# Applying the norm factor after the expert products instead of before them

## The chip, the cores and the metric

One Trainium2 chip; the kernel runs on one of its cores. The metric is the device time of one execution in microseconds (us). Engines: TensorE (PE, with its weight loads as PEld), VectorE (DVE), ScalarE (ACT), GpSimd (POOL) and SyncE (SP), which here only issues DMA.

## The reference

One encoder layer over 512 tokens of width 1024, float32. The first half is attention in three head groups, an output projection `w_out` and a residual. The second half, which the change is about, in short:

```
x = x + mix @ w_out                     # (512, 1024), called x1 in the kernel
h = x * rsqrt(mean(x*x) + eps) * g_ffn  # RMS norm: one factor r per token, one gain per column
group, two experts of 8 in the group, and two gates per token, from h @ w_r1, h @ w_r2
for each token and each of its two experts e (32 experts):
    a = silu(h @ w1[e]) * (h @ w3[e])   # w1, w3: 1024 x 512
    x += gate * (a @ w2[e])             # w2: 512 x 1024
```

The factor r is one number per token, so (r * x) @ w = r * (x @ w): it may be applied to rows before the products or to their results behind them.

## The kernel before, in words

**Attention and output projection.** The first 355 us compute the three head groups. The product with `w_out` is made in eight pieces (row block `a` of 128 tokens, column half `n`); three are issued before routing, the last five (`LISTED`) inside it.

**Routing** (`route`, lines 1101 to 1277). For each of four row blocks `a`: `add_x` adds the projection to `x1` (DVE); `square` sums squares (ACT); `rows` turns x1 on PE (`turn_x`), copies it (`copy`, ACT), multiplies by the router weights (`logits_x`, PE, line 1132), and computes the factor r with `rstd_ops` into `rst[:, 3, a]`. `full` (line 1149) makes the normed rows `xr = r * x1` on ACT, and `store` writes them to the DRAM tile `xd` from POOL's DMA queue. `xr` lives in the granules `k0` (blocks 0 and 1) and `va` (blocks 2 and 3), which attention has left. `choose` picks group and experts on DVE, ranks tokens within experts on PE, and gives every token-expert pair a slot: expert pair `pr` (experts pr and pr + 16) has 128 slots, 64 for each. `first_gather` multiplies `xr` by the one-hot matrix `G` on PE and so gathers the first 512 columns of pair 0's rows without a DMA. `table` builds on PE the list of tokens and gates by slot. The one-hot comparisons and the small operations ahead of `table` are on POOL for blocks 0 to 2 and on DVE for block 3.

These steps are tasks of a planner (`task`, `run_tasks`): each has an engine, a cost in us and its dependencies; the planner takes next the task that can start soonest and, among equals, the one with the longest way to the end. It fixes the order on each engine only. At run time every engine goes through its list in that order and waits for what each instruction needs.

**Experts** (line 1334 to the end). For each of 16 expert pairs: `up` multiplies the 128 gathered rows by w1 and w3 (PE, line 1406, the two experts of a pair on the two halves of the array), silu on ACT (line 1462), the product with the w3 result on DVE (line 1475), four transposes and the copy `uT` (ACT, line 1482), the product with w2 (line 1494), the gate, and `combine`, which adds the results to x1 through one-hot products (lines 1421 to 1424). `turn_rows` turns the rows of the next pair on PE. These rows come from `xd` by an indirect DMA of POOL (`rows_load`, line 1367), two pairs ahead; `rows_in` has two buffers.

**Weights.** The experts' 192 loads of 1 MB each are issued on SP in a fixed order by `load_w`, into a ring of 21 buffers named in `RING`; load n takes the buffer of load n - 21 and waits until it is free. Nine loads are issued during the output projection, twelve behind `route`, two more before the first pair, then two after every four k steps of products. SP issues in order: a load that waits for its buffer holds those behind it. The first nine are places `w` to the second `g` of the ring. Pair 0's half `up_half(0, 0, 0)` uses loads 1 and 2.

An overflow branch at the end (an expert with more than 64 tokens) reads `xd` too; it isn't entered with this input.

Of the kernel before, what the change touches and what calls it, by code (L numbers as in the profile page):

```python
# [12 lines left out]
F32 = mybir.dt.float32  # L13
# [4 lines left out]
AF = mybir.ActivationFunctionType  # L18
ALU = mybir.AluOpType
# [4 lines left out]
P = 128  # L24
S = 512
D = 1024
KT = D // P
# [5 lines left out]
F = 512  # L33
EPS = 1e-6
NEG = -1e30
RING = "w b q k2 k1 h h g g v f m m h h d e j k k0 va".split()
LN_EXP = [s.name for s in SETS].index("natural_log_exp_and_others")

NA_KEYS = ((64, 248), (0, 248), (0, 248), (0, 192))
# [5 lines left out]
def tile_encoder(ctx: ExitStack, tc, x, mem, g_mix, g_mem, g_ffk, w_in, w_kv, w_out, gains,  # L45
                 na_tab, dil_tab, w_r, b_r, w1, w3, w2, out):
    nc = tc.nc
    V = nc.vector
    cst = ctx.enter_context(tc.tile_pool(name="cst", bufs=1))
    drp = ctx.enter_context(tc.tile_pool(name="drp", bufs=1, space=DR))  # L50
    gov = drp.tile([S, NE], F32, name="gov")
    xd = drp.tile([S, D], F32, name="xd")
    man = ExitStack()
    man.enter_context(tc.manual_schedule())

    def xtile(name, n=D):
# [11 lines left out]
        name=nc.get_next_instruction_name(), engine=mybir.EngineType.Activation, ins=[], outs=[],  # L68
# [5 lines left out]
    ident = cst.tile([P, P], F32, name="ident")  # L74
# [6 lines left out]
    def granule(kind, name, dt=F32):  # L81
        return big.tile([P, 4, 512], dt, name=name, tag=kind, bufs=BUFS[kind])
# [800 lines left out]
    q = pt("warm")  # L883
# [12 lines left out]
    q = rows_turn(0)  # L896
# [117 lines left out]
    x1 = xtile("x1")  # L1014
# [4 lines left out]
    def small(name, shape, dt=F32):  # L1019
        return rk.tile(shape, dt, name=name)  # L1020
# [7 lines left out]
    rst = small("rst", [P, 4, 4])  # L1028
# [20 lines left out]
    def G_tile():  # L1049
        return rk.tile([P, 4, P], F32, name="G", tag="G", padded_shape=[P, 8, P])  # L1050

    xr, xr2, Gs, first_x = [], [], [], []


    class Task:
# [9 lines left out]
    def task(eng, dur, fn, *deps):  # L1065
        tasks.append(Task(eng, dur, fn, deps))
        return tasks[-1]
# [31 lines left out]
    LEAD = 1.0  # L1099

    def route():
        x_done, sq_done, lgt_done, free_lg, tb_done, pt_free, rl_done, mb_done, wop_prev, f_done = {}, {}, {}, {}, {}, [], {}, {}, [], {}

        parts, last_p, x_got = {}, [], {}

# [8 lines left out]
        def rows(a):  # L1114
            st = {}

            def turn_x(n):
                st["q", n] = bank("pt", NPT, "tTp")
                for k in range(4):
                    c = n * 512 + k * P  # L1120
                    nc.tensor.transpose(st["q", n][:, k * P:(k + 1) * P], x1[:, a, c:c + P], ident)

            def copy(n):
                if "tT" not in st:
                    st["tT"] = r3.tile([P, 2, 512], F32, name="tT", tag=("qTm", "kvm")[a % 2])
                nc.scalar.activation(st["tT"][:, n], st["q", n], AF.Copy)

            def logits_x(n):
                if n == 1:
                    st["l"] = bank(f"lg{a % 2}", 1, "rl")  # L1130
                for k in range(4):
                    nc.tensor.matmul(st["l"][:, 0:36], st["tT"][:, n, k * P:(k + 1) * P], wr[:, 4 * n + k, :],
                                     start=(n == 1 and k == 0), stop=(n == 0 and k == 3))
            rl = None
            for n in (1, 0):
                t = task("P", 0.46, lambda n=n: turn_x(n), x_done.get((a, n)), *pt_free[-NPT:][:1] if len(pt_free) >= NPT else ())
                c = task("A", 0.57, lambda n=n: copy(n), t, rl_done.get(a - 2))
                pt_free.append(c)
                rl = task("P", 0.95, lambda n=n: logits_x(n), c, rl, *free_lg.get(a - 2, ()))
            rl_done[a] = rl  # L1140
            s = rst[:, :, a:a + 1]
            r = s[:, 3]
            w = [task("V", 0.07, lambda: V.tensor_add(s[:, 0], sqs[:, a, 0:1], sqs[:, a, 1:2]), sq_done.get((a, 0)), sq_done.get((a, 1)))]
            for eng, dur, f in rstd_ops(s):
                w.append(task(eng, dur, f, w[-1]))
            r_done = w[-1]
            lgt = task("V", 0.17, lambda: V.scalar_tensor_tensor(lg[:, a], st["l"][:, 0:36], r, br, op0=ALU.mult, op1=ALU.add), rl, r_done)

            def full():
                if a % 2 == 0:  # L1150
                    xr2.append(granule(("k0", "va")[a // 2], "xr"))
                xr.append(xr2[a // 2][:, 2 * (a % 2):2 * (a % 2) + 2].rearrange("p a b -> p (a b)"))
                nc.scalar.activation(xr[a], x1[:, a], AF.Copy, scale=r)

            def store():
                nc.gpsimd.dma_start(xd[a * P:(a + 1) * P], xr[a])
            f_done[a] = task("A", 1.1, full, r_done, f_done.get(a - 1))
            task("G", 1.0, store, f_done[a])
            choose(a, lgt)

        def choose(a, lgt):
# [83 lines left out]
            def first_gather():  # L1245
                if a == 0:
                    first_x.append(bank("pj", 2, "xq"))
                for k in range(4):
                    nc.tensor.matmul(first_x[0][:, k * P:(k + 1) * P], xr[a][:, k::KT], Gs[0][:, a],
                                     start=(a == 0 and k == 0), stop=(a == 3), skip_group_check=True)  # L1250
            x_got[a] = task("P", 0.9, first_gather, G_last[-1], f_done[a], x_got.get(a - 1), last_p[0], x_done[LISTED[-2]])

            def table():
                if a == 0:
# [18 lines left out]
        for a in range(4):  # L1273
            block[0] = a
            rows(a)
        task("P", 3.0, lambda: None, x_got[3])
        run_tasks()

# [61 lines left out]
    att_stack.close()  # L1340
    wk_ = moe.enter_context(tc.tile_pool(name="wk", bufs=1, side="right", reuse_waits="tile"))
    rings["v"] = rings["f"] = wk_
    for tag, n, bufs in (("u", 2, 1), ("ringf", 8, 1), ("ringv", 8, 1), ("xT", 2, 4), ("rows", 4, 2), ("uT", 2, 1)):
        for _ in range(bufs):
            wk_.tile([P, n * 256], F32, name="place", tag=tag, bufs=bufs)
    load_w(12)
    ots = rk.tile([P, 2, 4, P], F32R, name="ot", tag="G")

    def scale_x(q, half):
        xT = wk_.tile([P, 4, P], F32, name="xT", tag="xT", bufs=4)  # L1350
        V.tensor_tensor(xT, q, gfk[:, 0, 4 * half:4 * half + 4].unsqueeze(2).to_broadcast([P, 4, P]), op=ALU.mult)
        return xT
# [5 lines left out]
    V.scalar_tensor_tensor(none, tb[0][:, 0:16], -1.0, none, op0=ALU.add, op1=ALU.add)  # L1358
    where_ = small("where", [P, 16], U32)
    V.tensor_copy(where_, none)  # L1360
    rows_in = [wk_.tile([P, D], F32, name="rows", tag="rows", bufs=2) for _ in range(2)][::-1]

    def rows_load(pr):
        if pr < 2:
            nc.gpsimd.memset(rows_in[pr], 0.0)
        if pr < NPAIR:
            nc.gpsimd.indirect_dma_start(out=rows_in[pr % 2], out_offset=None, in_=xd,  # L1367
                                         in_offset=bass.IndirectOffsetOnAxis(ap=where_[:, pr:pr + 1], axis=0),
                                         bounds_check=S - 1, oob_is_err=False)

# [19 lines left out]
    def turn_rows(pr, halves=range(2)):  # L1390
        nxt = []
        for half in halves:
            q = trp("xTp")
            for k in range(4):
                nc.tensor.transpose(q[:, k], rows_in[pr % 2][:, 4 * half + k::KT], ident)  # L1395
            nxt.append(scale_x(q, half))
        rows_load(pr + 2)
        return nxt

# [51 lines left out]
    def gate_half(pr):  # L1451
        if pr:
            p1 = up(pr, 0)
        else:
            p1 = up_tile(0)
            p_first.append(up_tile(1))
            up_half(0, 0, 0, p1)
            up_half(0, 1, 0, p_first[0])
            xT.extend(turn_rows(0, (1,)))
            up_half(0, 0, 1, p1)  # L1460
        u = wk_.tile([P, F], F32, name="u", tag="u", bufs=1)
        nc.scalar.activation(u, p1, AF.Silu)  # L1462
        return u

    def hidden(pr, u):

        nonlocal xT
        while pr == NPAIR - 1 and between:
            between.pop(0)()
        if pr:  # L1470
            p3 = up(pr, 1)
        else:
            p3 = p_first[0]
            up_half(0, 1, 1, p3)
        V.tensor_mul(u, u, p3)  # L1475
        if pr + 1 < NPAIR:
            xT = turn_rows(pr + 1)
        t = trp("uTp")
        for f in range(4):
            nc.tensor.transpose(t[:, f, :], u[:, f::4], ident)  # L1480
        uT = wk_.tile([P, 4, P], F32, name="uT", tag="uT", bufs=1)
        nc.scalar.activation(uT, t, AF.Copy)  # L1482
        while between:
            between.pop(0)()
        return uT
# [83 lines left out]
    with tc.If(flag > 0):  # L1569
        with tc.tile_pool(name="ov", bufs=1) as ov, tc.tile_pool(name="ovps", bufs=1, space=PS) as ovs:  # L1570
            with tc.For_i(0, NE) as e:
# [6 lines left out]
                for a in range(4):  # L1578
                    gv = ov.tile([P, 1], F32, name="gv")
                    nc.sync.dma_start(gv, gov[a * P:(a + 1) * P, bass.ds(e, 1)])  # L1580
                    t = ov.tile([P, D], F32, name="ovt")
                    nc.sync.dma_start(t, xd[a * P:(a + 1) * P])
                    o = ov.tile([P, D], F32, name="ovo")
                    nc.sync.dma_start(o, x_rows(out, a))
                    tT = ov.tile([P, KT, P], F32, name="ovtT")
                    for k in range(KT):
                        q = ovs.tile([P, P], F32, name="ovq1")
                        nc.tensor.transpose(q, t[:, k::KT], ident)
                        V.tensor_scalar_mul(tT[:, k], q, gfk[:, 0, k:k + 1])
                    hp = []  # L1590
                    for w in range(2):
# [86 lines left out]
```

## Time and profile before

| | |
|---|---|
| median of 3 runs | 855.46 us (853.81 to 856.22) |
| the profiled execution | 854.02 us |
| its span, first to last instruction | 852.2 us |
| PE busy | 804.7 us (94%) |
| DVE, ACT, POOL busy | 419.0, 256.3, 153.8 us |
| mean DMA rate over the span | 286 GB/s |

The span is the profiled execution's own; what it is short of the time lies before its first and behind its last instruction. Times in rows count from the start of the span. A busy PE is not PE at its peak, and the mean DMA rate joins an attention half that moves little with an expert half that moves nearly everything, so neither share says what bounds a stage.

### The profile page before, as it was taken

What the parts mean: (1) busy time and instruction counts of PE and PEld (TensorE: products, weight loads), DVE (VectorE), ACT (ScalarE), POOL (GpSimd) and SP (SyncE); (2) the same over time, 40 slices, a digit from 0 to 9 for tenths busy, and PEclk for the clock granted to TensorE, in tenths of its full rate; (3) what the DMA queues carried; (4) which work ended last, traced back from release to release, by engine and by line L of the source; (5) the groups of instructions that cost most, each with busy time, mean ns of one, the idle gap of its engine ahead of it and who ended that gap; (6) DMA issues with size and microseconds to landing.
All of it is one profiled execution on the core that took longest, in us unless ns stands there. A gap on an engine that the chain in (4) does not pass through costs nothing. (4 is left out here: it accounts for less than half of the span.)

```text
span 852.2 us, 12647 instructions
## 1 busy us (share of the span) xinstructions
PE 804.7 (94%) x4730; PEld 506.6 (59%) x4730; DVE 419.0 (49%) x1200; ACT 256.3 (30%) x768; POOL 153.8 (18%) x156
## 2 busy tenths in 40 slices
PE   7889999999989999998999999999998899889995
PEld 7879888879868867794344434444344334324433
DVE  6787798357759757563233224433143134214333
ACT  4666665565544544351110101101000000000001
POOL 5453322333232224133000000000000000000000
PEclk8899999999999999997999999999999999999999
DMA  9233212213122267897999999999999999999994
GB/s 332 60 105 95 64 51 62 89 50 121 50 72 72 72 178 294 356 416 276 425 426 425 427 424 426 427 425 427 425 426 427 425 426 426 425 430 425 428 397 140
DMA packets 65857, 243.78 MB, mean 286 GB/s; under 512 B 9072, under 2 KB 33648, under 8 KB 41984
## 3 DMA queue, kind: packets, MB, share of 16 engines
q1 hardware_dynamic: 55376, 230.18, 67.1%
q10 hardware_dynamic: 7504, 6.38, 3.0%
q0 software_dynamic: 2912, 6.36, 2.0%
q8 instruction: 39, 0.64, 0.3%
q14 instruction: 26, 0.21, 0.1%
HBM read 242.84 MB, written 4.26 MB: 290 GB/s over the span
## 5 line engine op out<-in xcount | busy, mean ns | idle before, releaser
L1406 PE MATMUL h<-w,xT 128*64 128x512 f32 x1024 | 235.6, 600 | 17.3 <-DMA w<-in_w_dram 15.8
L1406 PEld LDWEIGHTS h<-w,xT 128*64 128x64 f32 x1024 | 77.5, 138 | 170.2 <-issue 132.1
L1475 DVE TENSOR_TENSOR u<-u,h 128x512 f32<-128x512 f32 x16 | 11.0, 688 | 209.2 <-PE h L1406 209.2
L1494 PE MATMUL y<-w,uT 128*64 128x512 f32 x480 | 106.3, 595 | 0.7 <-ACT uT L1482 0.7
L199 POOL TENSOR_TENSOR wp<-wc,wp 128x512 fp32r<-128x512 f32 x51 | 66.9, 1315 | 129.8 <-ACT wp L198 105.2
L242 PE MATMUL pj<-wp,hTh 128*128 128x256 f32 (+1 forms) x268 | 79.7, 297 | 1.3 <-ACT hTh L786 1.0
L243 PE MATMUL pj<-wp,hTh 128*128 128x256 f32 (+1 forms) x268 | 77.3, 288 | 0.4 <-POOL wp L199 0.4
L244 PE MATMUL pj<-wp,hTl 128*128 128x256 f32 (+1 forms) x268 | 77.1, 288 | 0.2 <-DVE hTl L789 0.2
L1424 DVE TENSOR_TENSOR x<-x,c 128x512 f32<-128x512 f32 x120 | 73.1, 682 | 8.0 <-PE c L1422 6.5
L1367 POOL DMA_INDIRECT rows<-xd,where x16 | 16.1, 1003 | 320.7 <-PE xTp L1395 175.6
L1494 PEld LDWEIGHTS y<-w,uT 128*64 128x64 f32 x480 | 33.1, 137 | 65.9 <-issue 64.1
L1499 ACT ACTIVATE yh<-y,gate 128x512 fp32r<-128x512 f32 x30 | 20.6, 687 | 138.7 <-PE y L1494 137.6
L1500 DVE SCALAR_TENSOR_TENSOR yl<-y,gate,yh 128x512 fp32r<-128x512 f32 x30 | 22.5, 751 | 74.2 <-ACT yh L1499 74.2
L242 PEld LDWEIGHTS pj<-wp,hTh 128*128 128x128 f32 (+1 forms) x268 | 52.1, 194 | 4.1 <-issue 1.4
L1482 ACT ACTIVATE uT<-uTp 128x512 f32<-128x512 f32 x16 | 9.6, 598 | 146.0 <-PE uTp L1480 146.0
L243 PEld LDWEIGHTS pj<-wp,hTh 128*128 128x128 f32 (+1 forms) x268 | 52.1, 195 | 0.8 <-POOL wp L199 0.8
L244 PEld LDWEIGHTS pj<-wp,hTl 128*128 128x128 f32 (+1 forms) x268 | 52.1, 195 | 0.4 <-DVE hTl L789 0.4
L1421 PE MATMUL c<-yh,ot 128*128 128x512 f32 x120 | 48.6, 405 | 0.0
L1422 PE MATMUL c<-yl,ot 128*128 128x512 f32 x120 | 47.4, 395 | 0.0
L1462 ACT ACTIVATE u<-h 128x512 f32<-128x512 f32 x16 | 9.6, 597 | 117.5 <-PE h L1406 117.5
L242 PE MATMUL pj<-wq,hTh 128*128 128x256 f32 (+1 forms) x124 | 37.4, 301 | 2.8 <-ACT raw L289 2.8
L243 PE MATMUL pj<-wq,hTh 128*128 128x256 f32 (+1 forms) x124 | 35.4, 286 | 0.0
(319 smaller groups left out, 1425.9 us busy)
## 6 DMA issues: line engine op xcount, KB each, us to landing
w<-in_w_dram SPq DMA_DIRECT2D x188, 1024.0 KB, 19.6
wc<-in_w_in_dram SPq DMA_DIRECT2D x15, 1024.0 KB, 5.1
wo<-in_w_out_dram SPq DMA_DIRECT2D x4, 1024.0 KB, 4.8
w<-in_w_dram SPq DMA_DIRECT2D x6, 512.0 KB, 10.7
wc<-in_w_kv_dram SPq DMA_DIRECT2D x2, 1024.0 KB
x<-in_x_dram ACTq DMA_DIRECT2D x4, 512.0 KB, 10.4
xd<-xr POOLq DMA_DIRECT2D x4, 512.0 KB, 9.1
nab<-in_na_tab_dram ACTq DMA_DIRECT2D x8, 248.0 KB, 7.4
```

The lines of the kernel that those rows point to most:

```text
L199: (eng or nc.gpsimd).tensor_sub(dst[1], src, dst[0])
L242: nc.tensor.matmul(o, th, self.hi[k], start=(k == 0), stop=False)
L243: nc.tensor.matmul(o, th, self.lo[k], start=False, stop=False)
L244: nc.tensor.matmul(o, tl, self.hi[k], start=False, stop=(k == KT - 1))
L1367: nc.gpsimd.indirect_dma_start(out=rows_in[pr % 2], out_offset=None, in_=xd, in_offset=bass.IndirectOffsetOnAxis(ap=where_[:, pr:pr + 1], ...
L1406: nc.tensor.matmul(p[h * 64:(h + 1) * 64, :], xT[k // 4][:, k % 4, h * 64:(h + 1) * 64], wt[pr, w, q, h][:, k % 4, :], start=(k == 0), sto ...
L1421: nc.tensor.matmul(c, ot[:, a], yh, start=True, stop=False)
L1422: nc.tensor.matmul(c, ot[:, a], yl, start=False, stop=True)
L1424: V.tensor_add(sl, sl, c)
L1494: nc.tensor.matmul(y[h * 64:(h + 1) * 64, :], uT[:, f, h * 64:(h + 1) * 64], rows_of(wt[pr, 2, q, h])[:, f % 2, n * 512:(n + 1) * 512], st ...
L1499: nc.scalar.activation(yh, y, AF.Copy, scale=gate[:, pr:pr + 1])
L1500: V.scalar_tensor_tensor(yl, y, gate[:, pr:pr + 1], yh, op0=ALU.mult, op1=ALU.subtract)
```

## The change

Rows go to the experts without the norm. `full` and its granules are gone; the stores write `x1` into the first 1024 columns of `xd`, as soon as x1 is summed, and the first gather multiplies x1 itself. `xd` has one more column; a new DMA on POOL, behind all four blocks' factors, writes r there (512 single elements). A fetched row is 1025 elements long and brings its factor into column 1024 of `rows_in` (padded to 1032). `turn_rows` copies that column to `rs` on ACT, silu takes it as its scale, and the product with the w3 result becomes a three-operand instruction with it. `k0` and `va`, free earlier now, move in the ring from its end to the places behind the first nine loads. The overflow branch scales its rows itself.

```diff
-RING = "w b q k2 k1 h h g g v f m m h h d e j k k0 va".split()
+XW = 1032
+RING = "w b q k2 k1 h h g g k0 va v f m m h h d e j k".split()
...
-    xd = drp.tile([S, D], F32, name="xd")
+    xd = drp.tile([S, D + 1], F32, name="xd")
...
-            def full():
-                if a % 2 == 0:
-                    xr2.append(granule(("k0", "va")[a // 2], "xr"))
-                xr.append(xr2[a // 2][:, 2 * (a % 2):2 * (a % 2) + 2].rearrange("p a b -> p (a b)"))
-                nc.scalar.activation(xr[a], x1[:, a], AF.Copy, scale=r)
-
             def store():
-                nc.gpsimd.dma_start(xd[a * P:(a + 1) * P], xr[a])
-            f_done[a] = task("A", 1.1, full, r_done, f_done.get(a - 1))
-            task("G", 1.0, store, f_done[a])
+                nc.gpsimd.dma_start(xd[a * P:(a + 1) * P, 0:D], x1[:, a])
+            task("G", 1.0, store, x_done.get((a, 0)), x_done.get((a, 1)))
+            r_dones.append(r_done)
...
-                    nc.tensor.matmul(first_x[0][:, k * P:(k + 1) * P], xr[a][:, k::KT], Gs[0][:, a],
+                    nc.tensor.matmul(first_x[0][:, k * P:(k + 1) * P], x1[:, a, k::KT], Gs[0][:, a],
...
+        task("G", 1.0, lambda: nc.gpsimd.dma_start(xd.rearrange("(a p) c -> p a c", p=P)[:, :, D:D + 1], rst[:, 3].unsqueeze(2)), *r_dones)
...
-    rows_in = [wk_.tile([P, D], F32, name="rows", tag="rows", bufs=2) for _ in range(2)][::-1]
+    rows_in = [wk_.tile([P, XW], F32, name="rows", tag="rows", bufs=2) for _ in range(2)][::-1]
+    rs = small("rs", [P, 2])
...
-            nc.gpsimd.indirect_dma_start(out=rows_in[pr % 2], out_offset=None, in_=xd,
+            nc.gpsimd.indirect_dma_start(out=rows_in[pr % 2][:, 0:D + 1], out_offset=None, in_=xd,
...
-                nc.tensor.transpose(q[:, k], rows_in[pr % 2][:, 4 * half + k::KT], ident)
+                nc.tensor.transpose(q[:, k], rows_in[pr % 2][:, 4 * half + k:D:KT], ident)
             nxt.append(scale_x(q, half))
+        nc.scalar.activation(rs[:, pr % 2:pr % 2 + 1], rows_in[pr % 2][:, D:D + 1], AF.Copy)
         rows_load(pr + 2)
...
-        nc.scalar.activation(u, p1, AF.Silu)
+        nc.scalar.activation(u, p1, AF.Silu, scale=rs[:, pr % 2:pr % 2 + 1])
...
-        V.tensor_mul(u, u, p3)
+        V.scalar_tensor_tensor(u, p3, rs[:, pr % 2:pr % 2 + 1], u, op0=ALU.mult, op1=ALU.mult)
```

## Rows read from the trace of the kernel before

**Rows 1.** The page: busy share of the DMA engines in 40 slices, in tenths.

```profile
DMA  9233212213122267897999999999999999999994
```

**Rows 2.** Windows: stretch, its length, busy us by engine, granted clock, DMA share, GB/s.

```profile
385.00:390.00 5.00, 3.36 (x25) 3.15 (x21) 4.39 (x37) 1.77 (x6) 1.62 (x4) 0.77 0.93 390
390.00:395.00 5.00, 4.47 (x16) 3.08 (x18) 2.27 (x15) 0.41 (x1) 1.56 (x2) 0.50 0.37 98
395.00:400.00 5.00, 5.00 (x18) 1.41 (x16) 0.00 (x0) 0.00 (x0) 2.49 (x3) 0.70 0.65 226
750.00:800.00 50.00, 45.41 (x205) 17.51 (x202) 10.80 (x17) 4.54 (x7) 0.00 (x0) 1.00 1.01 427
```

**Rows 3.** Waits of the DMA queue on SP, 400 to 853 us: total, times, longest.

```profile
SPq L954 <- DMA w<-in_w_dram: 197.2, 97, 2.7
```

**Rows 4.** Timeline of the SP queue at the hand-over: start, duration, issue.

```profile
384.24 0.33 SPq L954 DMA_DIRECT2D w<-in_w_dram  x1
...
392.26 0.33 SPq L956 DMA_DIRECT2D w<-in_w_dram  x1
...
399.12 0.80 SPq L956 DMA_DIRECT2D w<-in_w_dram  x2
```

**Rows 5.** Waits of the SP queue, 398 to 401 us.

```profile
SPq L956 <- PE h L1406: 6.5, 1, 6.5
```

**Rows 6.** Timeline of PE, 382 to 411 us.

```profile
382.02 2.14 PE L1249 MATMUL xq<-G,xr 128*128 128x128 f32 x8
384.00 0.98 PE L1132 MATMUL rl<-wr,tT 128*128 128x36 f32 x8
...
389.90 2.28 PE L1249 MATMUL xq<-G,xr 128*128 128x128 f32 x8 [1.04 <-DVE G L1214]
...
392.97 9.55 PE L1406 MATMUL h<-w,xT 128*64 128x512 f32 x32 [0.53 <-DVE xT L1351]
...
404.02 7.09 PE L1406 MATMUL h<-w,xT 128*64 128x512 f32 x32 [0.85 <-DVE xT L1351]
```

**Rows 7.** Timeline of ACT in routing.

```profile
375.13 0.63 ACT L1112 ACTIVATE junk<-x 128x512 bf16<-128x512 f32 x1 [0.50 <-DVE x L1108]
...
380.75 1.15 ACT L1153 ACTIVATE xr<-x,rst 128x1024 f32<-128x1024 f32 x1 [0.53 <-DVE rst L173]
381.80 0.58 ACT L1126 ACTIVATE tT<-tTp 128x512 f32<-128x512 f32 x1
```

**Rows 8.** Timeline of POOL, 380 to 425 us.

```profile
380.97 0.68 POOL L1242 TENSOR_SCALAR val<-places,scr 128x128 fp32r<-128x128 f32 x1
...
382.57 0.62 POOL L1156 DMA_DIRECT2D xd<-xr  x1
383.91 0.23 POOL L1228 TENSOR_TENSOR scr<-O 128x32 f32<-128x32 bf16 x1 [0.72 <-DVE O L1195]
...
386.36 1.26 POOL L1242 TENSOR_SCALAR val<-places,scr 128x128 fp32r<-128x128 f32 x2 [0.92 <-DVE scr L1239]
...
394.39 1.11 POOL L1367 DMA_INDIRECT rows<-xd,where  x1 [0.87 <-DVE gate L1376]
...
424.11 0.82 POOL L1439 DMA_DIRECT2D gov<-wkb  x1 [10.40 <-DVE ovp L1440]
```

**Rows 9.** The page: issues of the row stores, and median us to landing.

```profile
xd<-xr POOLq DMA_DIRECT2D x4, 512.0 KB, 9.1
```

**Rows 10.** DMA queue of POOL, 402 to 853 us: packets, MB, share.

```profile
q0 software_dynamic: 2048, 3.75, 2.2%
```

**Rows 11.** DMA queue of ACT while 512 factors are stored, 28 to 36 us.

```profile
q10 hardware_dynamic: 528, 0.00, 3.2%
```

**Rows 12.** Groups by line on ACT: a 128x1 operation (busy us, mean ns).

```profile
L168 ACT ACTIVATE rst<-rst 128x1 f32<-128x1 f32 x4 | 0.8, 205 | 0.6 <-DVE rst L167 0.6
```

**Rows 13.** The page: groups of VectorE on the products' results.

```profile
L1475 DVE TENSOR_TENSOR u<-u,h 128x512 f32<-128x512 f32 x16 | 11.0, 688 | 209.2 <-PE h L1406 209.2
...
L1500 DVE SCALAR_TENSOR_TENSOR yl<-y,gate,yh 128x512 fp32r<-128x512 f32 x30 | 22.5, 751 | 74.2 <-ACT yh L1499 74.2
```

More of the change, by code (lines that the diff above doesn't have):

```diff
@@ L1050, in G_tile @@
         return rk.tile([P, 4, P], F32, name="G", tag="G", padded_shape=[P, 8, P])
-    xr, xr2, Gs, first_x = [], [], [], []
+    Gs, first_x = [], []
     class Task:
@@ L1101, in route @@
     def route():
-        x_done, sq_done, lgt_done, free_lg, tb_done, pt_free, rl_done, mb_done, wop_prev, f_done = {}, {}, {}, {}, {}, [], {}, {}, [], {}
+        x_done, sq_done, lgt_done, free_lg, tb_done, pt_free, rl_done, mb_done, wop_prev, r_dones = {}, {}, {}, {}, {}, [], {}, {}, [], []
         parts, last_p, x_got = {}, [], {}
@@ L1248, in first_gather @@
                 for k in range(4):
-                    nc.tensor.matmul(first_x[0][:, k * P:(k + 1) * P], xr[a][:, k::KT], Gs[0][:, a],
+                    nc.tensor.matmul(first_x[0][:, k * P:(k + 1) * P], x1[:, a, k::KT], Gs[0][:, a],
                                      start=(a == 0 and k == 0), stop=(a == 3), skip_group_check=True)
-            x_got[a] = task("P", 0.9, first_gather, G_last[-1], f_done[a], x_got.get(a - 1), last_p[0], x_done[LISTED[-2]])
+            x_got[a] = task("P", 0.9, first_gather, G_last[-1], x_done.get((a, 0)), x_done.get((a, 1)), x_got.get(a - 1), last_p[0], x_done[LISTED[-2]])
             def table():
@@ L1342, in tile_encoder @@
     rings["v"] = rings["f"] = wk_
-    for tag, n, bufs in (("u", 2, 1), ("ringf", 8, 1), ("ringv", 8, 1), ("xT", 2, 4), ("rows", 4, 2), ("uT", 2, 1)):
+    for tag, n, bufs in (("u", 2, 1), ("ringf", 8, 1), ("ringv", 8, 1), ("xT", 2, 4), ("rows", XW / 256, 2), ("uT", 2, 1)):
         for _ in range(bufs):
-            wk_.tile([P, n * 256], F32, name="place", tag=tag, bufs=bufs)
+            wk_.tile([P, int(n * 256)], F32, name="place", tag=tag, bufs=bufs)
     load_w(12)
@@ L1580, in tile_encoder @@
                     nc.sync.dma_start(gv, gov[a * P:(a + 1) * P, bass.ds(e, 1)])
-                    t = ov.tile([P, D], F32, name="ovt")
-                    nc.sync.dma_start(t, xd[a * P:(a + 1) * P])
+                    t = ov.tile([P, D + 1], F32, name="ovt")
+                    nc.sync.dma_start(t, xd[a * P:(a + 1) * P, 0:D + 1])
+                    V.tensor_scalar_mul(t[:, 0:D], t[:, 0:D], t[:, D:D + 1])
                     o = ov.tile([P, D], F32, name="ovo")
@@ L1587, in tile_encoder @@
                         q = ovs.tile([P, P], F32, name="ovq1")
-                        nc.tensor.transpose(q, t[:, k::KT], ident)
+                        nc.tensor.transpose(q, t[:, k:D:KT], ident)
                         V.tensor_scalar_mul(tT[:, k], q, gfk[:, 0, k:k + 1])
```

## The prediction

> **What bounds the kernel now.** I read four views: the page's slices, the windows over the expert stage, the waits of the DMA queue, and the timelines of the engines where routing hands over to the experts. In the slices the DMA row stands at 9 or more from the twentieth slice to the last but one [rows 1]. Of those stretches one stands in the rows: from 750 to 800 us the DMA engines are busy for the whole window at 427 GB/s, while PE has 4.6 us of idle time in 50 [rows 2]. The queue's own waits say the same: from 400 us on, the loads of w1 and w3 alone wait 197.2 us in 97 places for earlier weight loads [rows 3]. So from about 402 us on the weights stream without a break and the end is the moment at which this stream starts, plus bytes by rate, plus a short tail. A change in the expert stage counts only if it moves the start of the stream, the DMA time in it, or the tail.
>
> The start is what the reader should look at. From 385 to 400 us the DMA share falls to 0.93, 0.37 and 0.65 [rows 2]: 0.35 + 3.15 + 1.75 = 5.25 us of idle DMA. Two loads stand beside that hole: the load for granule k0 goes out at 384.24, that for va only at 392.26, and the next two at 399.12 [rows 4]. k0 and va are the tail of the ring of 21 buffers, and they are late because the normed rows `xr` lie in them until they are stored and used. But what the loads at 399.12 wait for is something else: 6.5 us for PE's products of line 1406 [rows 5]. These are loads 22 and 23 of the list; they go into the buffers of loads 1 and 2, and PE frees those after its first eight k steps of the first expert pair. PE begins them at 392.97 [rows 6]. All 21 buffers are loaded or loading before that; the stream resumes when PE gives the first buffer back.
>
> **The change, part by part.**
>
> *Four scaled copies leave ScalarE* (line 1153), 1.15 us each [rows 7]: 4.6 us of ACT time. Is any of it on PE's path to 392.97? The first two run under PE's long products with w_out, and the third ends ahead of a sum of squares that still waits 0.50 us for VectorE [rows 7]. The last, at 380.75, holds back a copy of the turned row block by 0.3 to 0.5 us (that copy starts at 381.80 [rows 7]); its reader is the router product at 384.00, which stands on PE behind the first-gather product that runs from 382.02 for 2.14 us [rows 6]. PE would still be in that product. The order of these two is set by the planner: working its costs through by hand, without the copy the router product is ready 0.02 us after the gather product in planned time, so their order should stay. I take 0. Bounds: 0, and a gain of 2.1 us if the order tips.
>
> *The first gather reads x1 instead of xr*: same shape, same two operands, and it waited for the one-hot G, not for the copy (its last run at 389.90 [rows 6] shows a wait for G). 0.
>
> *k0 and va move up in the ring, from places 20 and 21 to 10 and 11.* Both 1 MB loads then queue behind load 9 instead of waiting for the stores of xd. That fills part of the hole from the front: today the stream without va runs out shortly before 390, and one load of 1 MB takes 2.46 us at 427 GB/s, so loads 1 to 21 end at about 392. It doesn't move 399.12, because the loads after it wait for PE, not for these two. So the idle time moves from before va to behind it. I take 0; the bounds are 0 and the whole hole, 5.25 us.
>
> *The four stores of x1 go out earlier*, when x1 is summed; the last one's sum of squares starts at 375.13 [rows 7], so the store goes from after 382 to about 375.2. They are DMA time ahead of the hole: 0.
>
> *The column store is new*: 512 factors of 4 bytes, one more issue on POOL. Nearest row: the store of the gate table, also 128 by 4 pieces, held POOL 0.82 us [rows 8]. The planner puts it behind the third small operation of block 1, so the two comparisons that follow (the first at 380.97 [rows 8]) wait about 0.82 us. The old last store (0.62 us) stood behind them and is gone, and POOL then sat idle for 0.72 us before block 2's first operation at 383.91 [rows 8]: 1.34 us of room. 0. If that cover were gone it would cost 0.82 us on the way to the gather of block 2. The first row fetch at 394.39 [rows 8] needs the column landed; issued at 381.8 it has 12.6 us, and a store of 512 KB took 9.1 [rows 9]. 0.
>
> *Row fetches carry 4100 bytes a row instead of 4096.* These lie in the saturated stretch, so DMA time counts in full. Queue 0 took 2.2% of 16 engines from 402 to 853 us, 9.9 us, with 2048 packets, almost all of 14 fetches [rows 10]. Low bound: 4 bytes in 4096, 0.01 us. If each row becomes two packets, the small one is nearest to the 4-byte stores of `rdr`: 528 packets took 3.2% of 8 us on 16 engines, 4.1 us of one engine, 7.8 ns each [rows 11]; 128 by 7.8 ns over 16 engines is 0.06 us a fetch, 0.9 us over 14. Far bound: the second packet costs what the first does, 9.9 us. The small store is the nearest row, and whether rows split at all no row shows; I take 0.5, about half of 0.9. The Trainium skill (DMA: Bandwidth & Descriptors, How a descriptor splits into AXI transactions) says that a transfer is cut at 256-byte boundaries and that bytes before an unaligned start are fetched too. By that a row of 4100 bytes at a pitch of 4100 takes 17 pieces where 4096 took 16, an estimate of 0.6 us on the 9.9, and the sum below would be 0.1 us higher; no run here shows it yet.
>
> *Per pair, ScalarE copies the factor* (128 by 1; such operations took 205 ns [rows 12]) ahead of the uT copy, under PE's twelve transposes. 16 times 0.2 us hidden; without the cover 3.3 us. Silu's scale comes with the instruction. *VectorE's product becomes a three-operand form*: 688 ns before, 751 ns for the form on line 1500 [rows 13], 0.06 us more. Each of the first 15 is behind a stream that doesn't wait for PE; uncovered it would be 0.9 us. In the last pair it is in the tail: +0.06.
>
> Sum: 0.5 + 0.06 = +0.6 us. The profiled execution took 854.02 us (span 852.2), so it would give 854.6; its time is 1.4 us below the median 855.46, and the forecast against the median is **856.0**.
>
> **The rivals.**
>
> *The hole is filled and the time falls.* If the end were simply total bytes by rate from 346 us on, loading k0 and va early would win the hole back: 855.5 − 5.25 = 850.2. For it: the hole exists and the two late loads wait for xd. Against it: the wait at 399.12 names PE [rows 5]. Chance 0.10.
>
> *PE passes the hand-over sooner.* From 390 to 395 us its granted clock is 0.50, the 1.2 GHz level, after a window in which PE was busy for 3.36 of 5 us [rows 2]. The first 32 products take 9.55 us and the next 32, at the full clock, 7.09 [rows 6]. If less waiting in routing keeps the clock up, or the planner's order tips, 2.1 to 2.5 us go: about 853.0. Against it: the gaps of PE there are VectorE's chain for G, which the change leaves alone. Chance 0.08.
>
> *The column store waits for the row stores.* They are interleaved in one DRAM tile; if the framework takes the column's address range to overlap them, POOL, in order, stands until the last store has landed: 375.8 + 9.1 [rows 9] = 384.9, and 385.7 with its issue. The comparison of 380.97 is then 4.7 us late; POOL makes up 0.62 + 0.72 + 0.92 of idle time [rows 8], and 2.5 us stay, on the table product that stands on PE ahead of block 3's ranks: 858.0. Chance 0.12. By the Trainium skill (DMA: Bandwidth & Descriptors, Anatomy of one DMA) a store from this queue takes 2.0 us plus bytes over 436 GB/s, an estimate of 3.2 us for 512 KB; by that it has landed before the column's turn and this rival costs nothing. The trace disagrees, with 9.1 us [rows 9], under a full weight queue.
>
> *The fetches get dear (the slower side).* The place is the saturated stage, the mechanism a second packet or unaligned reads for each row of 4100 bytes; it decides from 2.6 us, when the added part costs a quarter of the 9.9 us of now. Up to 865.9. For it: nothing hides DMA time there. Against it: 7.8 ns for the smallest packets. Chance 0.12.
>
> **How the numbers follow.** The forecast has 0.58, the rivals 0.10, 0.08, 0.12 and 0.12. 0.3%, or 2.6 us, is about what a measurement here tells from no change. Faster: the filled hole and half of the sooner hand-over, 0.14. Slower: half of the waiting column, three quarters of the dear fetches and a little of the forecast's own spread, 0.18. Same: 0.68. The range leaves out the filled hole and the upper part of the dear fetches, 0.19 in all: 852.2 to 859.5.
>
> **What would show it.** Right: the loads for k0 and va issued by 357 us, DMA busy until about 392 and then idle; the two loads behind them still issued near 399 and waiting for line 1406; PE's first product of line 1406 near 393; the last weight load and the end where they were; queue 0 still near 2048 packets and 2.2% in the long stretch. Wrong: the stream resuming clearly before 399 us, POOL idle near 381 waiting for a store of xd, twice the packets in queue 0, or less than 425 GB/s in the long stage.

## The result, and the profile after

The changed kernel takes 862.04 us in the median of six runs (861.05 to 863.85); the kernel before took 854.63 us in six runs beside it. The ratio is 1.0088 with a 95% interval of 1.0068 to 1.0108: about 7.5 us slower, where 0.6 us more was forecast and the range ended at 859.5. The profiled execution took 863.85 us with a span of 862.1. Two of all the executions behind this document, one of the kernel before and one of the first experiment's kernel, took about 1580 us; the medians and ratios are those of the others.

The page's slices of the changed kernel (DMA share in tenths, then GB/s), and the GB/s of the kernel before:

```profile
DMA  9233112223122277997999999999999999999994
GB/s 313 79 98 104 53 50 85 64 64 105 49 71 71 71 188 287 398 409 274 419 420 419 419 419 418 420 419 419 420 420 418 418 422 419 418 421 419 419 385 130
```

```profile
GB/s 332 60 105 95 64 51 62 89 50 121 50 72 72 72 178 294 356 416 276 425 426 425 427 424 426 427 425 427 425 426 427 425 426 426 425 430 425 428 397 140
```

The DMA row looks as before [rows 1]: saturated from the twentieth slice on. The row under it is the news: 418 to 422 GB/s in nearly every slice of the long stage, where it was 424 to 430. The windows, for the stretches that were shown of before:

```profile
385.00:390.00 5.00, 4.40 (x32) 4.30 (x31) 4.05 (x31) 0.84 (x5) 2.86 (x9) 1.00 1.02 405
390.00:395.00 5.00, 3.44 (x21) 2.92 (x21) 3.12 (x23) 0.20 (x1) 0.96 (x1) 0.51 0.81 336
395.00:400.00 5.00, 5.00 (x14) 1.42 (x12) 0.45 (x7) 0.20 (x1) 3.13 (x3) 0.50 0.19 56
750.00:800.00 50.00, 45.92 (x207) 19.14 (x207) 15.19 (x24) 4.91 (x9) 0.07 (x1) 1.00 1.01 420
```

From 750 to 800 us the DMA share is as full as before, 1.01, and the rate is 420 GB/s where it was 427 [rows 2]. The DMA engines are busy all the time and move less. The hole at the hand-over is still there: 0.81 and 0.19 now in the second and third window, where it was 0.37 and 0.65; it has moved behind, as forecast.

The SP queue's issues at the hand-over, and what the last of them waited for:

```profile
347.80 0.80 SPq L958 DMA_DIRECT2D w<-in_w_dram  x2
...
357.83 0.33 SPq L958 DMA_DIRECT2D w<-in_w_dram  x1
...
376.09 0.33 SPq L958 DMA_DIRECT2D w<-in_w_dram  x1
...
401.02 0.80 SPq L958 DMA_DIRECT2D w<-in_w_dram  x2
```

```profile
SPq L958 <- PE h L1405: 24.6, 1, 24.6
```

The row at 347.80 carries two loads, the ninth of the list and the one for k0; that for va goes out at 357.83; the last buffer of the ring is ordered at 376.09. Then the queue waits 24.6 us for line 1405, the up products, and goes on at 401.02. So the two loads are 36 and 34 us earlier than before [rows 4], and the loads behind the ring are not earlier at all, but 1.9 us later.

PE at the hand-over:

```profile
383.70 2.15 PE L1245 MATMUL xq<-G,x 128*128 128x128 f32 x8
385.69 0.98 PE L1134 MATMUL rl<-wr,tT 128*128 128x36 f32 x8
...
391.36 2.27 PE L1245 MATMUL xq<-G,x 128*128 128x128 f32 x8 [1.04 <-DVE G L1210]
...
394.41 10.01 PE L1405 MATMUL h<-w,xT 128*64 128x512 f32 x32 [0.53 <-DVE xT L1348]
...
405.92 7.09 PE L1405 MATMUL h<-w,xT 128*64 128x512 f32 x32 [0.85 <-DVE xT L1348]
```

The order is that of before [rows 6], the gather product ahead of the router product, and the first four rows are 1.4 to 1.7 us later. The same products of the attention half already ran 1.75 us later at 345 us (343.28 in the profiled execution of before), so routing itself lost nothing; the first 32 products took 10.01 us instead of 9.55, with the granted clock at its lower level for longer: it was 0.50 in the whole window from 395 to 400 us, where its mean was 0.70 before [rows 2].

POOL around the new column store, and the landing times of the whole execution:

```profile
377.09 0.61 POOL L1152 DMA_DIRECT2D xd<-x  x1 [0.88 <-DVE x L1110]
...
382.35 0.24 POOL L1231 TENSOR_TENSOR scr<-scr,gt 128x32 f32<-128x32 f32 x1 [1.46 <-DVE at L1205]
382.82 0.85 POOL L1272 DMA_DIRECT2D xd<-rst  x1 [0.23 <-DVE scr L1235]
...
385.61 0.24 POOL L1224 TENSOR_TENSOR scr<-O 128x32 f32<-128x32 bf16 x1 [0.31 <-DVE O L1191]
...
395.99 1.13 POOL L1365 DMA_INDIRECT rows<-xd,where  x1 [0.99 <-DVE gate L1374]
```

```profile
xd<-x POOLq DMA_DIRECT2D x4, 512.0 KB, 9.2
...
xd<-rst POOLq DMA_DIRECT2D x1, 2.0 KB, 6.4
```

The column store of 512 factors is issued at 382.82 for 0.85 us, behind the third small operation of block 1 as the planner's costs said, and it waited for VectorE, not for the row store that went out at 377.09 (such stores take 9.2 us to land). It lands 6.4 us later, well ahead of the first fetch at 395.99. Block 2's first operation follows at 385.61, 1.70 us later than before [rows 8], which is the shift that everything has here. Queue 0 in the long stretch, and the operations that the change touches in the expert stage (busy us, mean ns of one; the silu of the kernel before is the last row on ACT):

```profile
q0 software_dynamic: 2052, 3.76, 2.2%
```

```profile
L1461 ACT ACTIVATE u<-h,rs 128x512 f32<-128x512 f32 x16 | 11.0, 687 | 103.4 <-PE h L1405 103.4
...
L1395 ACT ACTIVATE rs<-rows 128x1 f32<-128x1 f32 x15 | 2.9, 193 | 0.0
```

```profile
L1462 ACT ACTIVATE u<-h 128x512 f32<-128x512 f32 x16 | 9.6, 597 | 117.5 <-PE h L1406 117.5
```

```profile
L1474 DVE SCALAR_TENSOR_TENSOR u<-h,rs,u 128x512 f32<-128x512 f32 x16 | 12.0, 751 | 214.7 <-PE h L1405 214.7
```

2052 packets and 2.2%: rows of 4100 bytes do not become two packets and cost nothing that the share shows [rows 10]. The silu with its scale takes 687 ns instead of 597. The three-operand product takes 751 ns, as read from line 1500 [rows 13]; what VectorE waited for ahead of it is PE alone, so the longer silu held nothing up.

So where did the time go? From the moment at which the stream resumes to the last additions to x1 on VectorE it is 444.1 us before (399.12 to 843.24) and 450.8 us after (401.02 to 851.79): 6.7 of the 9.9 us of span (the rest: the stream resumes 1.9 us later, and the stretch behind those additions is 1.3 us longer). That is the weight stream. Its queue in the same 360 us, 440 to 800, of the kernel before and of the changed kernel (packets, MB, share of 16 engines):

```profile
q1 hardware_dynamic: 20603, 150.06, 98.8%
```

```profile
q1 hardware_dynamic: 20260, 147.56, 98.8%
```

The share is the same, so each byte takes more of the engines' time; the bytes are 1.7% less; 1.7% of some 424 us of stream is 7.1 us.

### The profile page after: what moved, and what is told of

Same layout as the page of the kernel before. It is cut to its first block, busy times and chain, and to the rows that moved or that the text cites. A ratio compares the mean times of both kernels' runs of the same rounds, so it can differ in the third digit from the quotient of the medians.

```text
span 862.1 us, 12669 instructions
## 1 busy us (share of the span) xinstructions
PE 807.6 (94%) x4730; PEld 507.1 (59%) x4730; DVE 420.1 (49%) x1200; ACT 255.3 (30%) x780; POOL 154.8 (18%) x157
## 4 chain that ended last, share of the span: by engine, by line
PE 51%; DMA 31%; DVE 10%; issue 3%; POOL 2%; ACT 2%; SPq 0%; DVEq 0%; POOLq 0%; ACTq 0%
DMA w<-in_w_dram 26%; PE h L1405 14%; PE y L1493 7%; PE pj L244 4%; PE pj L245 3%; PE pj L246 3%; DMA nab<-in_na_tab_dram 2%; PE c L1420 2%; PE c L1421 2%; PE pj L254 1%; PE pj L255 1%; DMA wc<-in_w_in_dram 1%; PE pj L256 1%; PE xTp L1393 1%; DVE rw L295 1%
## 5 line engine op out<-in xcount | busy, mean ns | idle before, releaser
L1474 DVE SCALAR_TENSOR_TENSOR u<-h,rs,u 128x512 f32<-128x512 f32 x16 | 12.0, 751 | 214.7 <-PE h L1405 214.7
L1461 ACT ACTIVATE u<-h,rs 128x512 f32<-128x512 f32 x16 | 11.0, 687 | 103.4 <-PE h L1405 103.4
```

## The experiments

The first theory came from what the diff does beside its purpose. The new tile `rs` has 8 bytes a partition and takes a place of 32 in the pool that lies in front of the big buffers. In the list of addresses of the two programs all 18 weight buffers behind it have moved, and with them their starts against multiples of 256 bytes, called the 256-byte grain from here on. That this lowers the rate is what the expectations call the placement theory. (The two buffers in "wk" moved because the fetched rows became wider.)

```
bytes behind a multiple of 256           before   changed kernel
14 buffers of "big", 4 of "ringd"           0          32
2 of "wk" (v, f)                          224         160
1 of "early" (w)                          224         224
```

**Aligned again.** The changed kernel with a larger `rs`:

```diff
-    rs = small("rs", [P, 2])
+    rs = small("rs", [P, 64])
```

> The changed kernel with the tile rs padded from 8 to 256 bytes a partition, so that 18 of the 21 weight buffers start at multiples of 256 bytes again, as before the change (in the changed kernel they start 32 bytes behind one). Placement theory: the DMA rate of the long stage goes back from 419 to about 426 GB/s and the time falls by about 6.5 us, from 862 to 855 or 856. Theory of the wide rows (4100 bytes a row in xd and in the fetches): the rate stays at 419 and the time near 862. Theory of the new ring order: the same, 862.

Measured: 855.02 us, ratio to the kernel before 1.0013 (0.9994 to 1.0033). The weight queue in 440 to 800 us, the windows at the hand-over, and a wait of the SP queue:

```profile
q1 hardware_dynamic: 20610, 150.07, 98.8%
```

```profile
365.00:370.00 5.00, 5.00 (x35) 4.48 (x34) 1.67 (x9) 3.08 (x9) 1.07 (x2) 1.00 0.48 198
370.00:375.00 5.00, 5.00 (x36) 4.48 (x36) 3.81 (x25) 1.17 (x6) 1.30 (x6) 1.00 0.26 105
375.00:380.00 5.00, 4.71 (x40) 4.48 (x39) 3.53 (x29) 2.88 (x12) 2.48 (x5) 1.00 0.94 304
385.00:390.00 5.00, 3.36 (x22) 3.15 (x21) 4.40 (x37) 0.90 (x5) 1.57 (x4) 0.76 1.00 407
390.00:395.00 5.00, 4.47 (x16) 3.02 (x18) 2.20 (x13) 0.00 (x0) 1.49 (x2) 0.50 1.01 426
395.00:400.00 5.00, 5.00 (x18) 1.41 (x16) 0.00 (x0) 0.00 (x0) 2.59 (x3) 0.71 1.01 422
```

```profile
SPq L956 <- PE wop L1300: 17.0, 1, 17.0
```

The bytes are back and so is the time; neither the wide rows nor the ring order can hold the loss. But there is a second thing to see. The hole isn't where the changed kernel had it: from 385 to 400 us the DMA runs full, and it idles at 365 to 375 instead. The load for buffer f waited 17.0 us for the products with w_out, and held those behind it: 256 bytes more on the left made f's place touch one that those products still read. So this kernel has a delay of its own, and two of the runs of the change below were made without it.

**The move alone.** The kernel before with an idle tile and nothing else:

```diff
     where_ = small("where", [P, 16], U32)
+    idle = small("idle", [P, 2])
+    nc.gpsimd.memset(idle, 0.0)
```

> The kernel before with one idle 8-byte tile beside the others, which moves the same 18 weight buffers by 32 bytes and does nothing else. Placement theory: 419 GB/s in the long stage, time 861 to 862. Both other theories: no change, 855.

Measured: 861.96 us, ratio 1.0088 (1.0061 to 1.0114), the loss of the whole change. Its queue from 440 to 800 us and its window:

```profile
q1 hardware_dynamic: 20270, 147.63, 98.9%
```

```profile
750.00:800.00 50.00, 45.78 (x207) 18.09 (x206) 12.78 (x21) 4.55 (x7) 0.00 (x0) 1.00 1.01 419
```

**64 and 128 bytes instead of 32**, with an idle tile of 16 and of 32 columns.

> The same with a 64-byte idle tile: the buffers start 64 bytes behind a multiple of 256. If only the 64-byte grain counts: 855, as before. If a start off the 256-byte grain costs (a piece more per row): 861 to 862, as with 32 bytes. Other theories: 855.

> The kernel before with a 128-byte idle tile: 18 weight buffers start 128 bytes behind a multiple of 256. If the grain is 256 bytes, it costs what 32 and 64 bytes cost: 860.5 to 862, 419 to 420 GB/s. If the grain is 128 bytes: 854, 426 GB/s.

Measured: 860.86 us, ratio 1.0080 (1.0053 to 1.0107), for 64 bytes, and 861.0, 1.0088 (1.0063 to 1.0114), for 128. All three offsets cost 0.8 to 0.9%, and the whole 256 bytes of the first experiment cost nothing that can be told: the grain that counts is 256 bytes. In bytes 32 is a little dearer: its queue moved 147.63 MB in 440 to 800 us, those of 64 and 128 moved 147.99 each.

**The wide rows alone.** The kernel before with what the change does to `xd` and to the fetches, but with normed rows:

```diff
-    xd = drp.tile([S, D], F32, name="xd")
+    xd = drp.tile([S, D + 1], F32, name="xd")
...
+        task("G", 1.0, lambda: nc.gpsimd.dma_start(xd.rearrange("(a p) c -> p a c", p=P)[:, :, D:D + 1], rst[:, 3].unsqueeze(2)), *r_dones)
...
-            nc.gpsimd.indirect_dma_start(out=rows_in[pr % 2], out_offset=None, in_=xd,
+            nc.gpsimd.indirect_dma_start(out=rows_in[pr % 2][:, 0:D + 1], out_offset=None, in_=xd,
```

> The kernel before with only the wide rows: xd has 1025 columns, a column store of the factors behind the row stores, fetches of 1025 elements into rows of 1032; the normed rows, the ring order and the 18 buffers' places stay as before. Placement theory: 855 to 856.5. Theory of the wide rows: 860 to 862, at 419 GB/s. Theory of the ring order: 855.

Measured: 855.13 us, ratio 1.0012 (0.9993 to 1.0032). The rival of the dear fetches falls.

**The old ring order, in the padded kernel.** The line `RING` of before in the kernel of the first experiment.

> The changed kernel with rs padded to 256 bytes and with k0 and va back at the end of the ring. Theory of the hand-over (loads behind the ring wait for PE, so loading k0 and va early only moves the idle time of the DMA): the loads for k0 and va go out later, by up to 30 us, and the time stays that of the aligned changed kernel, 855.4 (at most 0.5 us off). Rival, that the early loads win something which another cost of the change eats: 2 to 5 us slower, 857 to 860.

Measured: 860.12 us, ratio 1.0069 (1.0052 to 1.0086), 5.1 us more than with the new order by the medians, 4.8 by the ratios. Its windows:

```profile
360.00:365.00 5.00, 5.00 (x26) 4.17 (x25) 0.97 (x2) 1.45 (x4) 0.00 (x0) 1.00 0.26 107
365.00:370.00 5.00, 5.00 (x36) 4.48 (x33) 1.95 (x8) 2.99 (x8) 0.77 (x2) 1.00 0.26 105
370.00:375.00 5.00, 5.00 (x35) 4.48 (x34) 3.52 (x25) 1.42 (x8) 1.62 (x6) 1.00 0.27 108
375.00:380.00 5.00, 4.72 (x37) 4.48 (x37) 3.88 (x29) 2.85 (x11) 2.53 (x5) 1.00 0.89 283
```

Taken alone this speaks for the rival, and the hand-over theory would fall. But both kernels have the delay of f: their DMA idles 6.6 us (new order, 365 to 380 us) and 11.6 us (old order, 360 to 380), and then runs at 0.97 or more of its share in every window up to 440 us. 5.0 us less idle time and about 5 us less time agree: in them the stream is late, and early loads count in full. That is not the changed kernel's case, so the pair was made again without the delay.

**No buffer moved.** The changed kernel with `rs` in spare columns of a tile that has its 32 bytes anyway:

```diff
-    onef = small("onef", [P, 1])
+    onef = small("onef", [P, 3])
...
-    rs = small("rs", [P, 2])
+    rs = onef[:, 1:3]
```

> The changed kernel with rs in two spare columns of the 32-byte place that the tile onef has anyway: no buffer moves, 18 of 21 weight buffers are on the 256-byte grain, and the load for buffer f is not held up as it was by the 256-byte padding. Placement theory: 426 GB/s and 853.9 to 855.1, the time of the kernel before (the forecast for the change without the moved buffers was 0.6 us more than before). Rival, that the change wins time of its own which the padding hid by holding f: 849 to 852. Rival, that something else of the change costs: above 857.

> The same with k0 and va back at the end of the ring. Hand-over theory (once the ring is full the next load waits for PE, so the order inside the ring does nothing): the time of the kernel with the new order, within 0.7 us. Rival, that loading k0 and va early wins: 2 to 5 us slower than with the new order.

Measured: 855.3 us, ratio 1.0012 (0.9998 to 1.0026), with the new ring order, and 855.93, 1.0017 (1.0004 to 1.0029), with the old one. The weight queue, the windows and the wait of the kernel with the new order:

```profile
q1 hardware_dynamic: 20604, 150.06, 98.8%
```

```profile
390.00:395.00 5.00, 3.90 (x22) 3.67 (x21) 2.90 (x22) 0.34 (x2) 0.11 (x1) 0.50 0.61 257
395.00:400.00 5.00, 4.54 (x12) 1.46 (x14) 1.43 (x10) 0.00 (x0) 3.41 (x4) 0.50 0.17 48
750.00:800.00 50.00, 45.56 (x206) 17.80 (x204) 10.61 (x17) 4.90 (x9) 0.00 (x0) 1.00 1.01 427
```

```profile
SPq L958 <- PE h L1405: 26.5, 1, 26.5
```

The full rate, the hole behind the ring, and the queue waiting 26.5 us for line 1405: the forecast's picture, at the forecast's price (1.0 us more than before, with an interval of -0.2 to +2.2, so it can't be told from 0). The two ring orders lie 0.6 us apart, inside their intervals. So where the hand-over waits for PE, the order inside the ring does nothing that can be measured.

**How many buffers.** Two kernels that put the last three on the grain as well (224 bytes left free at the right end), then two with an idle tile of 32 bytes between the buffers of the kernel before:

```diff
+    ctx.enter_context(tc.tile_pool(name="edge", bufs=1, side="right")).tile([P, 56], F32, name="edge")
     rings = {"w": ctx.enter_context(tc.tile_pool(name="early", bufs=1, side="right"))}
```

```diff
+    big.tile([P, 8], F32, name="pad", tag="pad", bufs=1)
     turns = [(pr, w) for pr in range(NPAIR) for w in range(3)]
```

> The kernel before with 224 bytes left free at the right end of SBUF, so that the other three weight buffers (32 bytes off the 256-byte grain until now) start on it too. Placement theory, with some 7 us for 18 buffers, 0.39 us each: 1.2 us less than before, 852.7, rate 427 GB/s. If only a misplacement of most buffers costs (a limit that 3 of 21 don't reach): no change, 853.9.

> The changed kernel with all 21 weight buffers on the 256-byte grain (rs of 256 bytes, rows of 1056 elements, 224 bytes free at the right end). Placement theory: 1.2 us less than the changed kernel with 18 aligned buffers, 854.2; its rest (row fetches, factor copies, hand-over) stays as it is there. If the three don't matter: 855.4.

> The kernel before with a 32-byte idle tile between the weight buffers, so that 11 of 21 start off the 256-byte grain (3 before, 21 in the changed kernel). If every misplaced load costs for itself (7 us for 18): 3.1 us more, 857.1. If the write side has spare rate when placed well, which must be used up before anything is lost (an estimate from 426, 419 and 435 GB/s puts that at 12 buffers): no change, 854.

> The same with the idle tile further ahead, 15 of 21 off the grain. Each load for itself: 4.7 us more, 858.7. Spare rate of the write side: 2.3 us more, 856.3, at 424 GB/s.

Measured, with the MB that the weight queue moved from 440 to 800 us in one profiled execution of each (the kernel before took 854.2 us in the runs beside the two middle kernels, 854.0 in those beside the first):

| buffers off the grain | kernel | MB | time, us | ratio to the kernel before |
|---|---|---|---|---|
| 0 of 21 | before, all placed | 150.09 | 853.9 | 0.9999 (0.9988 to 1.0010) |
| 3 | before | 150.06 | 854.0 | |
| 11 | before, idle tile late | 149.29 | 855.44 | 1.0022 (1.0006 to 1.0039) |
| 15 | before, idle tile early | 148.63 | 859.17 | 1.0069 (1.0053 to 1.0086) |
| 21 | before, moved by 32 bytes | 147.63 | 861.96 | 1.0088 (1.0061 to 1.0114) |

The queue's rows of the two middle kernels:

```profile
q1 hardware_dynamic: 20499, 149.29, 98.8%
```

```profile
q1 hardware_dynamic: 20407, 148.63, 98.8%
```

The changed kernel with all 21 on the grain (`rs` of 256 bytes, rows of 1056 elements, the free 224 bytes; it has the delay of f too) took 856.04 us, 1.0019 (1.0007 to 1.0031), no better than with 18. Three buffers off the grain lose nothing: 0.03 MB of 150. From there the loss grows: 0.77 MB at 11, 1.43 at 15, 2.43 at 21. "Every load for itself" would have moved the first step by 0.4 MB, and its 1.2 us lie outside that kernel's interval; a spare of twelve buffers is wrong too, since 11 already lose 0.5% of the bytes and 15 cost 5.0 us by the medians, 5.9 by the ratio, where 2.3 were expected. Something between: a small spare that a few misplaced buffers use up.

The number of buffers leaves out their order in the ring, and the traces show that the order counts. They hold the time of every packet of the weight queue; taken by their starts, 128 packets of 8 KB are one load. From 440 to 800 us a packet takes 309 ns in over 99% of cases with 0 and with 3 buffers off. With 11 off, the misplaced buffers follow each other in runs of two and of seven; longer packets are 5% in the first load of such a run, 25% in the second, 63% in the third and about 90% in the fourth to the sixth. With 15 off (runs of two, six and seven) they are 15, 63 and 91% in the first three; with all 21 off by the move of 32 bytes they are 92%, and the mean packet is 5 to 6 ns longer. So the loss sits in loads that follow other misplaced loads: the first of a run is cheap, and the runs of one and two that the kernel before has are nearly free, with longer packets in 1 and 2% of cases. What holds this reserve no run shows.

## Why the prediction was wrong

**The step that failed** is the first: "the end is the moment at which this stream starts, plus bytes by rate, plus a short tail". The form held, and I went through moment, bytes and tail, but took the rate as given: 427 GB/s, read from the kernel before [rows 2], where the changed kernel has 420. The part "Per pair, ScalarE copies the factor" counted the instruction and gave its new tile no cost; that tile moved 18 of 21 weight buffers off the 256-byte grain and took 1.7% of the stream's bytes per time, 7 us or a little more of the 7.5. The same move without any of the change costs the same, and the change without the move costs 1.0 us, which can't be told from 0: shown from both sides. The sentence that named "less than 425 GB/s in the long stage" as a sign against the forecast was the one to come true.

The Trainium skill's rule that I used for the fetched rows (DMA: Bandwidth & Descriptors, How a descriptor splits into AXI transactions) comes nearest to this: a transfer that doesn't start on a multiple of 256 bytes is cut into one piece more. The trace agrees that the grain is 256 bytes, since offsets of 32, 64 and 128 all cost 0.8 to 0.9%. The section words it for bytes that are fetched, and doesn't say whether it holds for the place in SBUF that is written; in the kernel with the move alone only that place moved, and that more pieces are the reason no run shows. By the rule an 8 KB row would take 33 pieces for 32, an estimate of 3.1%; measured are 1.7% with all buffers off and nothing with three, so the measurement decides. For the fetched rows, where I had drawn it in, no cost can be seen.

**What held**, by the prediction's own parts:
- *Four copies leave ScalarE*: 0. The products of routing keep their order, and their distance within 0.3 us.
- *k0 and va move up*: 0. In the changed kernel the hole moved behind them, and the resumed stream waited for line 1405; with the buffers in place the old order is within 0.6 us of the new. The rival of the filled hole is refuted there, and the padded pair shows when it would be right: when the DMA, not PE, is late at the hand-over.
- *Column store*: 0. It waited for no row store, so that rival is refuted; 0.85 us for 0.82.
- *Fetches*: no second packet. The 0.5 us taken for them can't be told from zero.
- *Silu's scale comes with the instruction*: wrong as a price, 687 ns for 597, but hidden: VectorE's product behind it waits for PE alone.
- *Sum*: +0.6 us forecast for all of this, +1.0 measured without the moved buffers. Both lie within an interval that holds 0, so the terms of the sum are not confirmed one by one.
- *PE passes the hand-over sooner*: it didn't; the change does nothing to the wait for G. The 9.55 us of the first products were 10.01, 9.31 and 8.46 us in three of the profiled executions, with the granted clock falling to 0.50 at different moments, so 1 or 2 us of single executions hang on that.

The profiled execution of the changed kernel lies 1.8 us above its median. Some 1.75 us of its span were lost before 345 us, in attention, whose weights are loaded into the same moved buffers. Neither the move nor the change does it alone, by one execution of each: the fifth expert load goes out at 342.92 us before, at 344.16 in the changed kernel, at 341.98 in the kernel with the move alone and at 342.04 in the one with the change and no move. What it was stays open.

## What to carry to other kernels

A diff's allocations are part of the diff: before costing operations, list which buffers a new tile moves, and check the starts of those that a saturated DMA stream fills; here a tile of 8 bytes cost 7 us. Look at their order too: here the few misplaced loads of the kernel before cost next to nothing, and long runs of them cost in full. When a stage is bound by DMA, read share and GB/s together, since a full share at a lower rate was the mark of dearer transfers here, and not of waiting. Loading earlier pays only if the stream is what is late at the next hand-over: look at what the first load behind the full ring waits for.

## What the runs showed of the hardware

- The rate of 8 KB rows into SBUF depends on the 256-byte grain of their start: 426 GB/s with up to 3 of 21 buffers off it, 424 with 11, 422 with 15, 419 to 420 with 21, at a full DMA share each time. An 8 KB packet takes 309 ns on the grain, and 5 to 6 ns more on the mean where all 21 are off it; in a run of misplaced loads the first is cheap (longer packets in 1 to 15% of cases) and the full price (about 90%) comes from the third or fourth.
- An offset of 32, 64 or 128 bytes costs the same within the intervals (861.96, 860.86 and 861.0 us for 854).
- Silu on ACT takes 90 ns longer on 128x512 with a scale by partition than without (687 for 597 ns); one instruction more of 128x1 takes 193.
